# Half-size products for seven gate/up pairs, with weight sums made in DRAM

## The chip, the cores and the metric

The kernel runs on one NeuronCore of a Trainium2 chip. The metric is the device time of one execution in microseconds (us), given as the median of several runs. A profiled execution is one more run, recorded by the hardware profiler; its span, from the first to the last instruction, is what the profile's rows divide up. Engines are named as in the profile: PE is TensorE (matrix products), DVE is VectorE, ACT is ScalarE, POOL is GpSimd, SP is SyncE, whose queue issues nearly all transfers (DMAs). PEld is the loading of the stationary operand, which overlaps PE.

## The reference

One transformer block on 512 positions of width 1024, in fp32: normalize, project, attend in two ways (a sparse form with compressed, selected and windowed keys, and a sliding window with sinks), project, normalize, add; then the feed-forward part, which is what changes, and a gated addition at the end.

```python
h = rmsnorm(x, mlp_pre_g[i])
gu = h @ w_gate_up[i]                    # 1024 -> 2 x 2816
a, u = jnp.split(gu, [D_FF], axis=-1)
a = causal_dwconv(a, conv_w[i], conv_b[i])   # 3 taps along the positions
y = (jax.nn.gelu(a, approximate=True) * u) @ w_down[i]
x = x + rmsnorm(y, mlp_post_g[i])
e = p[i] @ w_ple[i]
x = x + e * jax.nn.sigmoid(x @ w_ple_gate[i])
```

## The kernel before

Everything is kept transposed: channels on the 128 partitions, the 512 positions along the free dimension (T = 512, H = 256, KC = 8 chunks of the model width, NFF = 22 tiles of the hidden width). A 32-bit product is made of three matmuls in a reduced 32-bit format (fp32r): each operand is split in a high part, a rounded copy made by ScalarE, and a low part, the difference, made by VectorE. The helper `mm3` (L149) issues high·high, low·high, high·low for one chunk of 128. The helper `weight` (L130) brings a weight tile of 128x1024 from DRAM (512 KB, on SP's queue, into a raw buffer "wr") and splits it (L134 on ScalarE, L138 on VectorE) into buffers "wh", of which there are six.

The program is written for a framework that assigns buffers and semaphores and orders each engine's instructions itself, by a simulated timeline; `prio`, `pin` and `keep_in_program_order` bend that order. The transfers of the SP queue share eight semaphores in rotation, so each waits until the one eight places before it has landed.

The stages in time: the input and its projections (to about 70 us); attention, in which the rest of the projections and the first half of the output projection run as fillers among the score and value products (`fill` at L180 is called once for each step of attention); output projection and norm (to about 279 us); gate/up (`mlp_up`, to about 494 us); down (`mlp_down`); the last norm and the gate.

Gate/up has 22 pairs j of tiles (gate and up, 24 matmuls of 512 columns each, 48 a pair). The input is not normalized beforehand: `self.h2` holds the un-normalized rows times the gain, split in high and low, and the normalization factor r3 (a row, spread over the partitions) is multiplied in behind the products, once for the gate tile (L1131, VectorE) and once for the up side (L1138, GpSimd). `mlp_tile` (below) does this with the three-tap convolution (L1134 to L1136), gelu (L1137), the product with the up tile (L1139) and the split of the result y (L1141, L1142). r3 itself is ready only after the first four tiles (`chunkwise`) and one more, so the first pairs queue up for it.

Down has eight output tiles c. Tiles 0 to 5 go as three pairs (`pair_of_tiles`): on the first 12 hidden tiles (6 pairs of them, KP = 6) a 2x2 block product is made with seven half-size products (Strassen's scheme: sums of weight blocks, sums of operand halves; 256 columns each), and the remaining ten hidden tiles go plainly. Tile 6 is plain, tile 7 is split in two halves of positions so that its norm can start early. The sums of operand halves are made by `sums` for the pairs of hidden tiles 0 to 3 (EARLY = 4) during gate/up, and by `sums_late` for the last two in down.

PSUM is eight banks of 128x512, handed out in rotation by tags ("mm" two, "s" three, "t" two, "o" one).

Of the kernel before, what the change touches and what calls it, by code (L numbers as in the profile page):

```python
# [64 lines left out]
EARLY = 4  # L65
MP = 3
ORDER = [[range(0, 4), (), range(4, 6)], [range(0, 3), range(3, 6), ()], [range(6), (), ()]]
TTAG = ["pt", "u", "u", "u", "p", "p", "p", "p"]
LAGS = [(1, 2), (2, 2)]


class Block:
# [76 lines left out]
    def mm3(self, ps, wt, off, x, start, stop, keep=False):  # L149
        mm = self.nc.tensor.matmul  # L150
        hi = wt[0][:, off : off + P]
# [5 lines left out]
        mm(ps, hi, x[:, 1, :], start=False, stop=stop)  # L157
# [876 lines left out]
    def sums(self, j, c):  # L1034

        nc = self.nc
        a, b = slice(0, H), slice(H, T)
# [4 lines left out]
        ta, tb = self.tt[j // 2]
        ra, rb = (self.sum[:, i, :] for i in range(2))
        if j % 2 == 0:
            nc.vector.tensor_sub(ra[:, a], c[:, b], c[:, a])
            nc.scalar.activation(rb[:, a], c[:, b], AF.Copy)
        else:
            nc.vector.tensor_sub(ra[:, b], c[:, b], ra[:, a])
            nc.vector.tensor_sub(rb[:, a], c[:, b], rb[:, a])
# [324 lines left out]
```

## Time and profile before

| what | us |
|---|---|
| median of three runs | 660.18 (659.74 to 660.29) |
| profiled execution, span | 657.9 |
| PE busy | 650.7 (99%) |
| DVE busy | 452.6 (69%) |
| ACT busy | 342.1 (52%) |
| POOL busy | 171.6 (26%) |
| share of PE in the chain that ended last | 93% |

A window row, as the prediction uses them, reads: the stretch and its length, then for PE, PEld, DVE, ACT and POOL the busy time and in brackets the number of instructions, then the granted TensorE clock, the busy share of the 16 DMA engines and the GB/s that they moved. A timeline row has the start, the duration, the engine, the line, the operation and what it writes and reads; in square brackets stands the idle time before it and who ended it. A row of a group has its busy time and the mean duration in ns behind the bar. A row on DMAs ends with the KB of each and the median us from issue to landing.

### The profile page before, as it was taken

What the parts mean: (1) busy time and instruction counts of PE and PEld (TensorE: products, weight loads), DVE (VectorE), ACT (ScalarE), POOL (GpSimd) and SP (SyncE); (2) the same over time, 40 slices, a digit from 0 to 9 for tenths busy, and PEclk for the clock granted to TensorE, in tenths of its full rate; (3) what the DMA queues carried; (4) which work ended last, traced back from release to release, by engine and by line L of the source; (5) the groups of instructions that cost most, each with busy time, mean ns of one, the idle gap of its engine ahead of it and who ended that gap; (6) DMA issues with size and microseconds to landing.
All of it is one profiled execution on the core that took longest, in us unless ns stands there. A gap on an engine that the chain in (4) does not pass through costs nothing.

```text
span 657.9 us, 9783 instructions
## 1 busy us (share of the span) xinstructions
PE 650.7 (99%) x3449; PEld 556.3 (85%) x3449; DVE 452.6 (69%) x965; ACT 342.1 (52%) x636; POOL 171.6 (26%) x248
## 2 busy tenths in 40 slices
PE   9999999999999999999999999999999999999997
PEld 8988878878888888888888888888889898989986
DVE  7795687978856469689876555555568857544873
ACT  7464687978887476346544333333334433342351
POOL 1111597677486060003211010101010002021000
PEclk9999999999999999999999999999999999999999
DMA  8436721212264437221242233222233332656032
GB/s 304 161 113 201 199 66 49 55 27 63 67 213 156 144 106 277 97 64 65 96 129 96 97 97 112 97 96 97 96 97 97 113 96 81 214 180 233 1 113 80
DMA packets 32129, 77.99 MB, mean 119 GB/s; under 512 B 3536, under 2 KB 11728, under 8 KB 32080
## 3 DMA queue, kind: packets, MB, share of 16 engines
q1 hardware_dynamic: 31936, 77.28, 36.7%
q8 instruction: 27, 0.44, 0.3%
q14 instruction: 22, 0.18, 0.1%
q10 hardware_dynamic: 144, 0.08, 0.0%
HBM read 63.72 MB, written 6.29 MB: 106 GB/s over the span
## 4 chain that ended last, share of the span: by engine, by line
PE 93%; DVE 4%; ACT 2%; POOL 1%; issue 1%; ACTq 0%; DVEq 0%
PE mlpup_pss L156 4%; PE mlpup_pss L153 4%; PE mlpup_pss L157 4%; PE mlpup_psmm L156 3%; PE mlpup_pst L156 3%; PE mlpup_psmm L153 3%; PE mlpup_pst L153 3%; PE mlpup_pst L157 3%; PE mlpup_psmm L157 3%; PE mlpdown_psmm L153 2%; PE mlpdown_psmm L157 2%; PE mlpdown_psmm L156 2%; PE mlpdown_pst L157 2%; PE mlpdown_pst L153 2%; PE mlpdown_pst L156 2%; PE nsa_pso L597 2%
## 5 line engine op out<-in xcount | busy, mean ns | idle before, releaser
L1138 POOL TENSOR_TENSOR mlpup_s<-mlpup_s,r3b 128x512 f32<-128x512 f32 x22 | 32.5, 1475 | 215.0 <-ACT mlpup_s L1137 215.0
L134 ACT ACTIVATE mlpup_wh<-mlpup_wr 128x1024 fp32r<-128x1024 f32 x38 | 40.1, 1057 | 61.8 <-PE mlpup_pss L156 27.6
L138 DVE TENSOR_TENSOR mlpup_wh<-mlpup_wr,mlpup_wh 128x1024 fp32r<-128x1024 f32 x38 | 46.4, 1222 | 4.5 <-ACT mlpup_wh L134 4.5
L153 PE MATMUL mlpup_pss<-r_u,mlpup_wh 128*128 128x512 f32 x120 | 46.7, 389 | 0.0
L156 PE MATMUL mlpup_pss<-r_u,mlpup_wh 128*128 128x512 f32 x120 | 46.7, 389 | 0.0
L157 PE MATMUL mlpup_pss<-r_u,mlpup_wh 128*128 128x512 f32 x120 | 46.7, 389 | 0.0
L587 POOL TENSOR_SCALAR nsa_u<-nsa_u,nsa_nrc,gate 128x512 f32<-128x512 f32 (+3 forms) x64 | 38.6, 615 | 14.7 <-DVE nsa_nrc L723 9.6
L134 ACT ACTIVATE mlpdown_wh<-mlpdown_wr 128x1024 fp32r<-128x1024 f32 (+2 forms) x22 | 21.3, 968 | 40.6 <-DMA mlpdown_wr<-in_down_dram 14.7
L689 ACT ACTIVATE nsa_u<-nsa_u,nsa_nnm 128x512 f32<-128x512 f32 (+3 forms) x64 | 35.4, 554 | 6.7 <-DVE nsa_nnm L682 6.6
L138 DVE TENSOR_TENSOR mlpdown_wh<-mlpdown_wr,mlpdown_wh 128x1024 fp32r<-128x1024 f32 (+2 forms) x22 | 24.4, 1111 | 20.7 <-ACT mlpdown_wh L134 20.7
L569 DVE TENSOR_TENSOR nsa_u<-nsa_pst,nsa_u 128x512 fp32r<-128x512 f32 (+1 forms) x43 | 29.4, 686 | 6.8 <-ACT nsa_u L566 6.5
L275 POOL TENSOR_TENSOR mlpdown_s<-mlpdown_s,mlpdown_s 128x512 f32<-128x512 f32 x6 | 9.8, 1630 | 93.0 <-ACT mlpdown_s L274 92.9
L138 POOL TENSOR_TENSOR fill_wh<-fill_wr,fill_wh 128x1024 fp32r<-128x1024 f32 (+2 forms) x13 | 24.6, 1896 | 26.5 <-ACT fill_wh L134 26.5
L1137 ACT ACTIVATE mlpup_s<-mlpup_s 128x512 f32<-128x512 f32 x22 | 13.9, 631 | 33.7 <-DVE mlpup_s L1136 33.7
L153 PE MATMUL mlpup_pst<-r_u,mlpup_wh 128*128 128x512 f32 x80 | 31.1, 389 | 0.0
L156 PE MATMUL mlpup_pst<-r_u,mlpup_wh 128*128 128x512 f32 x80 | 31.1, 389 | 0.0
L157 PE MATMUL mlpup_pst<-r_u,mlpup_wh 128*128 128x512 f32 x80 | 31.1, 389 | 0.0
L153 PE MATMUL mlpup_psmm<-r_u,mlpup_wh 128*128 128x512 f32 x80 | 31.1, 389 | 0.0
L156 PE MATMUL mlpup_psmm<-r_u,mlpup_wh 128*128 128x512 f32 x80 | 31.1, 389 | 0.0
L157 PE MATMUL mlpup_psmm<-r_u,mlpup_wh 128*128 128x512 f32 x80 | 31.1, 389 | 0.0
L682 DVE CUSTOM_DVE_ANT_0 nsa_u<-nsa_pss,biastables_u 128x224 f32<-128x224 f32 (+3 forms) x64 | 27.8, 446 | 3.0 <-PE nsa_pss L623 2.4
L566 ACT ACTIVATE nsa_u<-nsa_pst 128x512 fp32r<-128x512 f32 x43 | 25.4, 593 | 8.5 <-PE nsa_pst L564 7.9
(493 smaller groups left out, 2130.2 us busy)
## 6 DMA issues: line engine op xcount, KB each, us to landing
mlpup_wr<-in_gu_dram SPq DMA_DIRECT2D x38, 512.0 KB, 3.3
fill_wr<-in_win_dram SPq DMA_DIRECT2D x6, 512.0 KB, 3.7
mlpdown_u<-in_down_dram SPq DMA_DIRECT2D x11, 256.0 KB, 3.0
fill_u<-fill_u SPq DMA_DIRECT2D x20, 128.0 KB, 2.6
mlpdown_wr<-in_down_dram SPq DMA_DIRECT2D x5, 512.0 KB, 3.5
mlpdown_wr<-in_down_dram SPq DMA_DIRECT2D x6, 384.0 KB, 3.2
loadx_u<-in_xT_dram SPq DMA_DIRECT2D x8, 256.0 KB, 4.5
compress_u<-projk_u SPq DMA_DIRECT2D x16, 128.0 KB, 2.4
```

The costliest lines, as they stand in the source:

```text
L134: h = nc.scalar.activation(hi, raw, AF.Copy)
L138: l = eng.tensor_sub(lw, raw, hi.bitcast(F32))
L153: r = self.pin(mm(ps, hi, x[:, 0, :], start=start, stop=False))
L156: mm(ps, lo, x[:, 0, :], start=False, stop=False)
L157: mm(ps, hi, x[:, 1, :], start=False, stop=stop)
L566: nc.scalar.activation(t[:, 0, :], pt, AF.Copy)
L569: nc.vector.tensor_sub(t[rs, part, :], pt[rs], t[rs, 0, :].bitcast(F32))
L587: self.nc.gpsimd.tensor_scalar(ap, ap, col, gate, op0=ALU.mult, op1=ALU.mult)
L682: nc.vector.tensor_tensor_reduce(dst, src, dist, op0=ALU.add, op1=ALU.min, scale=SLOPES[8 + 4 * g + r], scalar=start, accum_out=out)
L689: nc.scalar.activation(dst, dst, AF.Exp, bias=nm[:, r, b : b + 1], scale=-1.0, accum_out=sm[:, r, b : b + 1])
L1137: nc.scalar.activation(c0, c0, AF.Gelu_apprx_tanh)
L1138: nc.gpsimd.tensor_mul(c0, c0, self.r3)
```

## The change

Seven of the gate/up pairs (j = 9, 11, ... 21) are computed by half-size products. For these, the four 4-chunk blocks of the pair (gate and up, first and second interleaved half of the input channels) and the two halves of the positions form a 2x2 block product with seven products of 4 chunks by 256 columns, 84 matmuls instead of 48 of 512 (`blocked_tile`). Further parts go with it:

- `normalized`: during the first gate/up tiles the input is multiplied by gain and r3 and split anew (`hn`), and the sums of its halves are made (`ht`). Tiles from j = 8 on use `hn` and no longer need the products with r3.
- The weight blocks come in a second layout of the same numbers (`gs`). Their sums are made in DRAM: 28 copies of 256 KB (four for each blocked pair) are issued on SP's queue during attention (`block_copies`), and 28 accumulating DMAs of 256 KB, two levels in a chain, on GpSimd's queue (`block_additions`).
- In down, the plain tile 6 comes first, and the operand sums of all six pairs are made there and in the first pair (`sums_of`); `sums`, `sums_late` are gone. The weights of the last gate are loaded behind the pairs.

```diff
-EARLY = 4
-ORDER = [[range(0, 4), (), range(4, 6)], [range(0, 3), range(3, 6), ()], [range(6), (), ()]]
+ORDER = [[range(0, 3), (), range(3, 6)], [range(0, 3), range(3, 6), ()], [range(6), (), ()]]
+BLOCKED = [9, 11, 13, 15, 17, 19, 21]
+ROWS = 2048
+RAW_LAST = 7
+COPY_FROM, COPY_STEP = 10, 3
...
         if self.loads:
             self.loads.pop(0)()
+        else:
+            self.calls += 1
+            if self.calls > COPY_FROM and self.calls % COPY_STEP == 0:
+                next(self.copies, lambda: None)()
...
+    def normalized(self, x1, kp):
+        f = self.u([P, 2, T])
+        for i in range(2):
+            k = 2 * kp + i
+            h = self.u([P, 2, T], F32R)
+            nc.vector.scalar_tensor_tensor(f[:, i, :], x1[kp][:, i, :], self.col(C_GMLP + k), self.r3, op0=ALU.mult, op1=ALU.mult)
+            nc.scalar.activation(h[:, 0, :], f[:, i, :], AF.Copy)
+            nc.vector.tensor_sub(h[:, 1, :], f[:, i, :], h[:, 0, :].bitcast(F32))
+            self.hn.append(h)
+            yield
+        t = self.u([P, 4, H])
+        parts = [self.u([P, 2, T], F32R, PTAG[2 * kp + i]) for i in range(2)]
+        self.half_sums([[f[:, i, hs] for hs in HALF] for i in range(2)], t, parts)
+        self.ht += parts
+        yield
+
+    def block_copies(self):
+        self.sums_in = [self.dp.tile([4, P, T], F32, name=f"blocks{i}") for i in range(len(BLOCKED))]
+        rows = lambda t: t.rearrange("p n -> (p n)").rearrange("(q e) -> q e", e=ROWS)
+        for i, d in enumerate(self.sums_in):
+            for k in range(4):
+                yield lambda i=i, d=d, k=k: self.load_late(rows(d[k]), rows(self.io["gs"][i, k]))
+
+    def block_additions(self):
+        nc, gs = self.nc, self.io["gs"]
+        rows = lambda t: t.rearrange("s p n -> s (p n)").rearrange("s (q e) -> q s e", e=ROWS)
+        add = lambda o, a: self.pin(nc.gpsimd.dma_start(rows(o), rows(a), accum_op=ALU.add, max_dma_last_dim=4 * ROWS))
+        for lo in range(0, len(BLOCKED), 2):
+            some = list(enumerate(self.sums_in))[lo : lo + 2]
+            for i, d in some:
+                yield lambda i=i, d=d: add(d[2:3], gs[i, 0:1])
+                yield lambda i=i, d=d: add(d[3:4], gs[i, 2:3])
+            for i, d in some:
+                yield lambda d=d: add(d[0:1], d[3:4])
+            for i, d in some:
+                yield lambda d=d: add(d[1:2], d[0:1])
+
+    def blocked_tile(self, j, tags):
...
+        plan = [
+            [(d[:, a], 0, x(0, a), True), (e[:, a], 4, x(1, a), True)],
+            [(f[:, b], 0, t(2), True), (g[:, b], 4, t(0), True)],
+            [(f[:, a], 0, t(1), False), (e[:, b], 4, x(1, b), False)],
+            [(g[:, a], 0, t(3), False)],
+        ]
+        for wt, products in zip(self.blocked_weights(j), plan):
+            for ps, first, op, begins in products:
+                for k in range(4):
+                    self.mm3(ps, wt, (first + k) * P, op(k), begins and k == 0, k == 3, shared=True)
+        q, v, w = self.s([P, T]), self.s([P, T]), self.s([P, T], tag="as")
+        nc.scalar.activation(q[:, a], d[:, a], AF.Copy)
+        nc.vector.tensor_sub(v[:, a], q[:, a], f[:, a])
+        nc.vector.tensor_add(v[:, b], v[:, a], f[:, b])
+        nc.vector.tensor_sub(q[:, b], v[:, a], g[:, b])
+        nc.vector.tensor_add(q, q, e)
...
+        self.conv(j, v, q)
+        nc.vector.tensor_mul(v, w, v)
+        self.keep_y(j, v)
...
     def mlp_down(self):
...
-        for c in range(0, 2 * MP, 2):
-            self.pair_of_tiles(c, yo[c // 2], acc)
         for c in range(2 * MP, KC - 1):
             m = yo[c // 2][:, c % 2, :]
             ps = self.ps("mm")
             for n, k in enumerate(ks):
                 wt = self.weight(io["down"][c][:, k.start * P : k.stop * P], len(k) * P)
                 self.gemm(ps, wt, [self.y[j] for j in k], k.start == 0, k.stop == NFF)
-                if n < 2:
-                    self.pgw.append(self.weight(io["wpg"][n], tag="u"))
+                self.sums_of(n)
...
+        for c in range(0, 2 * MP, 2):
+            self.pair_of_tiles(c, yo[c // 2], acc)
```

`sums_of(i)` adds the high and low parts of two hidden tiles (two additions of 512 columns), and `half_sums` makes four sums of 256 columns and splits them (two splits of 512).

How the order moves on three engines. First SP's queue in the attention stage, at about 59 to 73 us of the profile before. `fill_wr` are weight loads, `projq_u` moves of queries, `compress_u<-projk_u` the moves that fill the second half of the compressed keys, and `blocks` the DRAM buffers of the weight sums. Before:

```order
L146 DMA fill_wr_846<-in_win_dram 128x1024
L282 DMA projq_u_701<-projq_u_698 64x512 x4
L146 DMA fill_wr_1146<-in_win_dram 128x1024
L282 DMA compress_u_455<-projk_u_768 64x512 x2
L282 DMA compress_u_457<-projk_u_768 64x512
L282 DMA compress_u_456<-projk_u_768 64x512 x2
```

After:

```order
L156 DMA fill_wr_846<-in_win_dram 128x1024
L295 DMA blocks_975<-in_gs_dram 16x4096 x3
L298 DMA projq_u_701<-projq_u_698 64x512 x4
L295 DMA blocks_975<-in_gs_dram 16x4096
L295 DMA blocks_976<-in_gs_dram 16x4096
L156 DMA fill_wr_1159<-in_win_dram 128x1024
L295 DMA blocks_976<-in_gs_dram 16x4096 x2
L298 DMA compress_u_455<-projk_u_768 64x512 x2
L298 DMA compress_u_456<-projk_u_768 64x512 x2
```

Seven copies of 256 KB now stand ahead of the key moves, and the moves of tile 456 have come one place forward.

Second GpSimd, from the reciprocal root of the second norm on (r2c, at 243.94 in the profile before); the L1138 and, after, L1163 rows are the products with r3 for j = 0, 1, 2 and so on. Before:

```order
L222 TENSOR_TENSOR r2c<-r_rv_3059,mhalf 128x4
L1138 TENSOR_TENSOR mlpup_s_3347<-mlpup_s_3347,r3b 128x512
L1138 TENSOR_TENSOR mlpup_s_3363<-mlpup_s_3363,r3b 128x512
L1138 TENSOR_TENSOR mlpup_s_3406<-mlpup_s_3406,r3b 128x512
L1138 TENSOR_TENSOR mlpup_s_3472<-mlpup_s_3472,r3b 128x512
L1138 TENSOR_TENSOR mlpup_s_3552<-mlpup_s_3552,r3b 128x512
L1138 TENSOR_TENSOR mlpup_s_3630<-mlpup_s_3630,r3b 128x512
```

After, from the product for j = 3 to that for j = 5:

```order
L1163 TENSOR_TENSOR mlpup_s_3541<-mlpup_s_3541,r3b 128x512
L1199 DMA blocks_980<-in_gs_dram 32x2048 x2
L1199 DMA blocks_979<-blocks_979 32x2048
L1199 DMA blocks_980<-blocks_980 32x2048
L1199 DMA blocks_979<-blocks_979 32x2048
L1163 TENSOR_TENSOR mlpup_s_3646<-mlpup_s_3646,r3b 128x512
L1199 DMA blocks_980<-blocks_980 32x2048
L1199 DMA blocks_981<-in_gs_dram 32x2048 x2
L1199 DMA blocks_981<-blocks_981 32x2048 x2
L1163 TENSOR_TENSOR mlpup_s_3741<-mlpup_s_3741,r3b 128x512
```

Between these three products stand ten accumulating DMAs, and each `blocks<-blocks` waits for the one before it on the same buffer; twelve more stand between r2c and the product for j = 0, and six among the first products.

Third VectorE at the start of down, where the first two block weights (split in `mlpdown_wh` of 128x896) are made; L1058, L1131 to L1142 before are operand sums and the last hidden tiles. Before:

```order
L138 TENSOR_TENSOR mlpdown_wh_4841<-mlpdown_wr_4838,mlpdown_wh_4840 128x1024
L1142 TENSOR_TENSOR mlpup_u_4751<-mlpup_s_4744,mlpup_u_4751 128x512
L1131 TENSOR_TENSOR mlpup_u_3161<-mlpup_pss_4760,r3b 128x512
L1058 TENSOR_TENSOR mlpdown_s_4992<-mlpup_u_3875 128x512
L138 TENSOR_TENSOR mlpdown_wh_4875<-mlpdown_wr_4868,mlpdown_wh_4874 128x896
L1058 TENSOR_TENSOR mlpdown_s_4999<-mlpup_u_3948 128x512
L1058 TENSOR_TENSOR mlpdown_s_5008<-mlpup_u_4021 128x512
L1135 SCALAR_TENSOR_TENSOR mlpup_s_4817<-mlpup_u_3161,cols,mlpup_s_4817 128x512
L1136 SCALAR_TENSOR_TENSOR mlpup_s_4817<-mlpup_u_3161,cols,mlpup_s_4817 128x512
L138 TENSOR_TENSOR mlpdown_wh_4906<-mlpdown_u_4899,mlpdown_wh_4905 128x896
```

After:

```order
L148 TENSOR_TENSOR mlpdown_wh_5517<-mlpdown_wr_5510,mlpdown_wh_5516 128x896
L1153 TENSOR_TENSOR mlpup_u_5295<-mlpup_s_5282,mlpup_u_5295 128x512
L1062 TENSOR_TENSOR mlpdown_u_5382<-mlpdown_u_5383,mlpdown_u_5382 128x512
L1062 TENSOR_TENSOR mlpdown_u_5419<-mlpdown_u_5421,mlpdown_u_5419 128x512
L1062 TENSOR_TENSOR mlpdown_u_5420<-mlpdown_u_5421,mlpdown_u_5420 128x512
L1062 TENSOR_TENSOR mlpdown_u_5471<-mlpdown_u_5473,mlpdown_u_5471 128x512
L1062 TENSOR_TENSOR mlpdown_u_5472<-mlpdown_u_5473,mlpdown_u_5472 128x512
L1332 COPY mlpdown_u_5302<-mlpdown_psmm_5303 128x512
L148 TENSOR_TENSOR mlpdown_wh_5548<-mlpdown_u_5541,mlpdown_wh_5547 128x896
```

The splits of the operand sums (L1062) now stand between the first two block weights, behind the last hidden tile (5295).

More of the change, by code (lines that the diff above doesn't have):

```diff
@@ L1 @@
+import functools
 import itertools
@@ L95, in __init__ @@
         self.loads = []
+        self.calls = 0
+        self.copies = self.block_copies()
         self.pinned = None
@@ L156, in mm3 @@
         mm(ps, lo, x[:, 0, :], start=False, stop=False)
-        mm(ps, hi, x[:, 1, :], start=False, stop=stop)
+        self.last = mm(ps, hi, x[:, 1, :], start=False, stop=stop).ins
     def pin(self, r):
@@ L853, in attention @@
             self.fill_step()
+        for c in self.copies:
+            c()
         self.mix += [(mix[3][0][:, k, :], mix[3][1][:, k, :]) for k in range(2)]
@@ L1116, in pair_of_tiles @@
             plain(js)
+            if c == 0 and js is gs[0]:
+                for i in range(3, KP):
+                    self.sums_of(i)
             blocks(ks)
-            if c == 0 and js is gs[0]:
-                self.sums_late()
             if c == 2 * MP - 2 and len(ks):
@@ L1143, in mlp_tile @@
-        self.y.append(y)
-        if j < 2 * EARLY:
-            self.sums(j, c0)
+        c = self.s([P, T])
+        if j <= RAW_LAST:
+            a = self.s([P, T], tag="as")
+            nc.vector.tensor_mul(a, pa, self.r3)
+            self.conv(j, c, a)
+            nc.gpsimd.tensor_mul(c, c, self.r3)
+        else:
+            self.conv(j, c, pa)
+        nc.vector.tensor_mul(c, pu, c)
+        self.keep_y(j, c)
+    def normalized(self, x1, kp):
+        nc = self.nc
+        f = self.u([P, 2, T])
[12 more added lines that the diff above has]
+        yield
@@ new lines, in blocked_weights @@
+    def blocked_weights(self, j):
+        nc, i = self.nc, BLOCKED.index(j)
+        for src in (self.io["gs"][i, 0:2], self.sums_in[i][2:4], self.sums_in[i][0:2]):
+            yield self.weight(self.raw(src.rearrange("s p n -> p s n"), tag=next(self.rawtag)), early=True)
+        r = self.raw(self.io["gs"][i, 3], T, next(self.rawtag))
+        w = self.up.tile([P, D], F32R, tag="wh", name=self.nm("wh"), bufs=SLOTS["wh"])
+        hi, lo = (w[:, i * T : (i + 1) * T] for i in range(2))
+        nc.scalar.activation(hi, r[:, :T], AF.Copy)
+        nc.vector.tensor_sub(lo, r[:, :T], hi.bitcast(F32))
+        yield hi, lo
@@ L1167, in mlp_up @@
         nc, io = self.nc, self.io
-        am = self.u([P, 2, T + 2], F32, "kn")
-        self.am = [am[:, i, :] for i in range(2)]
-        for a in self.am:
-            nc.gpsimd.memset(a[:, 0:2], 0.0)
         self.y = []
         self.tt = []
-        ROT = self.ROT
+        self.hn, self.ht = [], []
+        x1 = self.x1
         pss = self.chunkwise(self.upw, self.h2, ("s", "mm", "s", "mm"))
@@ L1223, in mlp_down @@
         wts = []
-        for n, k in enumerate(ks):
-            wts.append(self.weight(io["down"][c][:, k.start * P : k.stop * P], len(k) * P))
-            if n == 0:
-                self.pgw.append(self.weight(io["wpg"][2], tag=("kn", "tt")))
+        for k, t in zip(ks, ("wr", "wr", "u")):
+            n = len(k) * P
+            wts.append(self.weight(self.raw(io["down"][c][:, k.start * P : k.stop * P], n, t), n, early=True))
+        for n, tag in enumerate((("p", "tt"), ("pt", "pt"), ("kn", "tt"))):
+            self.pgw.append(self.weight(io["wpg"][n], tag=tag))
         raw = self.raw(io["wpg"][3])
```

137 lines of the change are left out of this document (79 added, 58 removed).

## The prediction

> **What bounds the kernel now.** I read the engines' busy times first, then the chain that ended last, then the waits.
>
> ```profile
> span 657.9 us, 9783 instructions
> PE 650.7 (99%) x3449; PEld 556.3 (85%) x3449; DVE 452.6 (69%) x965; ACT 342.1 (52%) x636; POOL 171.6 (26%) x248
> PEclk9999999999999999999999999999999999999999
> PE 93%; DVE 4%; ACT 2%; POOL 1%; issue 1%; ACTq 0%; DVEq 0%
> PE x_psmm L303 <- DVE x_s L300: 1.5, 1, 1.5
> PE fill_psmm L863 <- POOL nsa_u L584: 0.3, 1, 0.3
> ```
>
> TensorE is busy for 650.7 of 657.9 us at the full granted clock, and its longest waits in the whole trace are 1.5 and 0.3 us. So time can only go by giving TensorE less to do, and a new wait of TensorE is added in full: no idle stretch swallows it later. For the same reason none of the costs bounded below can turn out a gain: there is no wait that could vanish. All sums below are made against this execution's span, 657.9; the median of the runs, 660.18, lies 2.3 above it, and I carry the difference over unchanged.
>
> **What the blocked pairs save.** The change replaces 48 matmuls of 512 columns by 84 of 256 in seven of the 22 gate/up pairs. Both shapes stand in the trace: 512 columns in the gate/up stage, 256 in the down stage's existing half-products. These two rows cover a stretch of each; the second count, PEld, is the number of weight loads, one for each matmul.
>
> ```profile
> 283.32:294.20 10.88, 10.88 (x49) 9.01 (x48) 8.97 (x13) 6.25 (x7) 1.30 (x1) 1.00 0.31 97
> 495.57:503.08 7.51, 7.51 (x64) 7.50 (x63) 7.48 (x17) 4.93 (x8) 0.00 (x0) 1.00 0.00 0
> ```
>
> 48 matmuls take 10.88 us, 0.2267 each; 63 half-width ones take 7.51, 0.1192 each, which is 53% and not 50%. Multiplication count alone promises an eighth of a pair, 1.36 us; the real saving is 10.88 − 84 × 0.1192 = 10.88 − 10.01 = 0.87 us, times seven **−6.1 us**. Nothing else on TensorE changes in number: the down stage does the same products in another order.
>
> **The r3 products that go** (14 on VectorE, 14 on GpSimd, for pairs 8 to 21) lie beside TensorE and are worth nothing in themselves: in steady state VectorE is busy 32, then 27 of 50 us (rows further down). The adds after each blocked pair (about 5.6 us of VectorE) and its four weight splits fit there: a blocked and a plain pair together need about 15 of VectorE's 20.9 us, and the four PSUM banks that a blocked pair takes come free a pair earlier. Cost 0.
>
> **The 28 copies on SP's queue.** They are put among the loads and moves of the attention stage, and seven of them stand ahead of the eight moves that fill the second half of the compressed keys (three after the load at 59.27, one before and one to three around the load at 65.10). Rows of SP's queue, of TensorE, and of the windows there (last two columns: share of the DMA engines, GB/s):
>
> ```profile
> 59.27 0.54 SPq L146 DMA_DIRECT2D fill_wr<-in_win_dram  x1
> 65.10 0.54 SPq L146 DMA_DIRECT2D fill_wr<-in_win_dram  x1
> 67.10 5.61 SPq L282 DMA_DIRECT2D compress_u<-projk_u  x8
> 72.70 0.40 PE L622 MATMUL nsa_pss<-compress_u,projq_u 128*128 128x512 f32 x1
> compress_u<-projk_u SPq DMA_DIRECT2D x8, 128.0 KB, 2.8
> 60.00:62.00 2.00, 2.00 (x12) 1.37 (x11) 0.60 (x1) 1.36 (x2) 1.07 (x1) 1.00 0.98 296
> 62.00:64.00 2.00, 2.00 (x10) 1.61 (x9) 1.97 (x2) 0.00 (x0) 1.33 (x1) 1.00 0.63 156
> 64.00:66.00 2.00, 2.00 (x10) 1.68 (x9) 1.54 (x6) 0.92 (x2) 0.00 (x0) 1.00 0.46 107
> 66.00:68.00 2.00, 2.00 (x10) 1.65 (x10) 1.41 (x2) 1.07 (x2) 0.00 (x0) 1.00 0.90 283
> 68.00:70.00 2.00, 2.00 (x11) 1.65 (x10) 0.41 (x1) 0.00 (x0) 0.00 (x0) 1.00 0.79 191
> 70.00:72.00 2.00, 2.00 (x12) 1.71 (x11) 1.53 (x6) 1.69 (x2) 0.77 (x1) 1.00 0.61 144
> 80.00:90.00 10.00, 9.75 (x60) 8.25 (x59) 7.88 (x44) 9.33 (x31) 9.35 (x16) 1.00 0.01 3
> ```
>
> The moves are issued from 67.10 on, 0.7 us apart, and land 2.8 us later. The score matmul at 72.70 reads two key tiles; their fourth half is the fifth move in line before, so it lands at about 67.1 + 4 × 0.7 + 2.8 = 72.7: no slack. After, it is the fourth, 0.7 us of slack. The DMA engines are free for 0.04 + 0.74 + 1.08 + 0.20 + 0.42 + 0.78 = 3.3 us between 60 and 72. At 0.90 share they moved 283 GB/s, so 314 at full share; a copy of 256 KB then takes 0.84 us of all engines if it costs what a load of that size does, and 1.7 if reading and writing DRAM count apart. Seven copies: 5.9 us against 3.3 free, 2.6 late, less 0.7: a **stall of 1.9 us**. No DRAM-to-DRAM row exists; the bounds are 0 (the three early ones go into the gap at 59 to 61 and the moves' waits for their sources hide the rest) and 7 × 1.7 − 3.3 − 0.7 = 7.9. I take 1.9, since the nearest rows are loads. The other 21 copies fall after these moves, where the engines rest (share 0.01 from 80 to 90) and the loads that they delay are needed later: 0.
>
> **The 28 accumulating DMAs on GpSimd's queue.** GpSimd runs in order. Twelve of them stand between the reciprocal root at 243.94 and the first r3 product, in 46 us in which GpSimd does nothing else: 0. The other 16 stand among the eight r3 products that stay, and there the second-level ones wait for the first to land.
>
> ```profile
> 243.94 1.95 POOL L222 TENSOR_TENSOR r2c<-r_rv,mhalf 128x4 f32<-128x4 f32 x1 [3.15 <-DVE r_rv L220]
> 292.53 1.30 POOL L1138 TENSOR_TENSOR mlpup_s<-mlpup_s,r3b 128x512 f32<-128x512 f32 x1 [46.65 <-ACT mlpup_s L1137]
> 303.96 1.31 POOL L1138 TENSOR_TENSOR mlpup_s<-mlpup_s,r3b 128x512 f32<-128x512 f32 x1 [2.55 <-ACT mlpup_s L1137]
> 340.55 0.69 DVE L1139 TENSOR_TENSOR mlpup_s<-mlpup_pst,mlpup_s 128x512 f32<-128x512 f32 x1 [2.07 <-POOL mlpup_s L1138]
> 348.61 0.39 PE L153 MATMUL mlpup_pss<-r_u,mlpup_wh 128*128 128x512 f32 x1
> kept_x<-outproj_u SPq DMA_DIRECT2D x2, 512.0 KB, 3.0
> kept_e<-pletiles_u SPq DMA_DIRECT2D x4, 512.0 KB, 7.2
> ```
>
> Between the fourth product (303.96 + 1.31 = 305.3) and the sixth stand ten of these DMAs with four waits for a landing in a row. With T from issue to landing and 0.54 us an issue (SP's, above) the sixth starts at 305.3 + 5.4 + 4T = 310.7 + 4T. VectorE then has its product with the up half and about 5.9 us of other rows before it splits the weight that TensorE takes at 348.61, so GpSimd may be as late as 348.6 − 5.9 − 0.7 − 1.3 = 340.7, which is T = 7.5. Stores to DRAM bound T: 3.0 to 7.2 us. Both ends are hidden; an accumulation also reads its target, so I do not exclude more. I take T = 5 and cost **0**, cover 10 us. [...]
>
> **VectorE from 279 to 355.** Here the pairs 0 to 7 still carry everything, and the normalized input and its half sums are added.
>
> ```profile
> 279.00:290.00 11.00, 11.00 (x50) 9.11 (x49) 10.47 (x11) 3.15 (x5) 0.00 (x0) 1.00 0.16 48
> 290.00:330.00 40.00, 40.00 (x178) 33.14 (x177) 36.23 (x54) 23.74 (x35) 11.13 (x6) 1.00 0.25 82
> 330.00:380.00 50.00, 50.00 (x222) 41.41 (x221) 32.33 (x43) 21.13 (x28) 6.71 (x5) 1.00 0.33 107
> 380.00:430.00 50.00, 50.00 (x223) 41.40 (x222) 27.00 (x35) 18.33 (x23) 6.46 (x5) 1.00 0.33 107
> L138 DVE TENSOR_TENSOR mlpup_wh<-mlpup_wr,mlpup_wh 128x1024 fp32r<-128x1024 f32 x36 | 44.0, 1222 | 3.0 <-ACT mlpup_wh L134 3.0
> L1135 DVE SCALAR_TENSOR_TENSOR mlpup_s<-mlpup_u,cols,mlpup_s 128x512 f32<-128x512 f32 x21 | 16.7, 795 | 0.3 <-ACT mlpup_s L1134 0.3
> L1142 DVE TENSOR_TENSOR mlpup_u<-mlpup_s,mlpup_u 128x512 fp32r<-128x512 f32 x20 | 13.7, 684 | 0.2 <-ACT mlpup_u L1141 0.2
> L1049 DVE TENSOR_TENSOR mlpup_u<-mlpup_s,mlpup_u 128x256 f32<-128x256 f32 x4 | 1.7, 414 | 0.0
> ```
>
> VectorE's load is 10.5 + 36.2 + half of 32.3 = 62.9 of 76 us. The sums of four early pairs go: 4 × (4 × 0.41 + 2 × 0.68) = 12.0. In come 8 scaled copies and 8 low parts, 8 × (0.80 + 0.68) = 11.8, and 16 half sums with 8 low parts, 16 × 0.41 + 8 × 0.68 = 12.1. Net +11.9: 74.8 of 76. Following its instructions in the changed order with these durations, the tightest weight (the one used at 348.6) is split about 2 us before. So there is cover, but a thin one: 0 to 3, taken **0.5 us**.
>
> **The start of down.** All six pairs' sums are now made here, 6 × (2 × 0.69 + 4 × 0.41 + 2 × 0.68) = 26 us of VectorE where before only two were late. The plain tile moved to the front and the first plain chunks cover it: about 87 matmuls, 19.7 us, plus 1 us until the first block's low weight is wanted; VectorE's 34 rows from the last blocked tile to that weight add up to about 20.6. Just in time, and then five low parts of sums (5 × 0.68) and a split of 896 columns, about 4.5 us, stand before the second block's weight, while a block gives TensorE 21 × 0.1192 = 2.5. That is 2 us late; the row at 495.57 above already shows VectorE at 7.48 of 7.51 in this place. Bounds 0 (the scheduler's order lets TensorE run ahead) and 4; taken **1.5 us**.
>
> The loads of the last projection's weights, moved behind the pairs, still have the split last tile as cover; the tail is 0.
>
> **Sum.** −6.1 + 1.9 + 0 + 0.5 + 1.5 = −2.2: span 655.7, median **658.0**.
>
> **Rivals.** (1) Everything is covered: 660.18 − 6.1 = 654.1. For it: each of the three stalls has 0 as its lower bound, and only the copies' one lies in a place where the moves land without slack. Against: VectorE at 75 of 76 us, and engines at 0.98, 0.90 and 0.79 share where the copies go. (2) The copies are dear: at 1.7 us each the stall at 72.7 is 7.9, and the time 660.2 − 6.1 + 7.9 + 2.0 = 664; from 5.4 us on it is slower than before beyond 0.2%, which I call the limit of what a measurement can tell. From 2.7 to 5.4 it shows no change. For it: TensorE uses the keys in the very moment at which they land. Against: the loads of this stage read DRAM and write elsewhere at 314 GB/s without paying twice. (3) The accumulations are slow. At T = 8.5 the sixth product starts at 344.7, 4 us late, VectorE stands behind it, TensorE behind VectorE's weight: 662; at T = 10 668. It decides from T = 8.4. For it: the landing of 7.2 us above; against: the other store row, 3.0, and a cover of 10 us at T = 5. [...] (4) The blocked matmuls do not reach 0.1192 because each product changes its bank: at 0.1296 the saving is 0, time 664 with the stalls; the down stage's half-products alternate banks at 0.1192, which speaks against it.
>
> **Chances.** Forecast, with 655.5 to 658.9 as its own range: 0.42. All covered: 0.17. Copies: 0.22, more than half of it no change, the rest slower. Accumulations: 0.15, nearly all slower. Half-products at no gain: 0.04, slower. Faster by over 0.2% is the first two, 0.59; within it 0.16; slower 0.25. The range runs from the covered case, less 0.4, to the copies' and the accumulations' dear cases, 664.
>
> **What the changed profile would show.** Blocked tiles at 10.0 us a pair; a wait of TensorE for a DMA of about 2 us near 72.7 (step two); no GpSimd product later than 340 and no VectorE wait for it over 2 us (step three); a wait of TensorE for VectorE under 1 us before 355 and of 1 to 2 us after the last blocked tile. The prediction is wrong if the first of these waits is absent (rival 1) or above 4 us (rival 2), or if GpSimd's sixth product starts after 345 (rival 3).

## The result: 0.7% slower, with five new waits

The changed kernel took 664.61 us (median of four runs, 662.78 to 666.63) against 659.96 of the kernel before in the same comparison; the ratio is 1.0071, 95% interval 1.0051 to 1.0091. The prediction, 658.0 with a range to 664.0, was too low, and it forecast a gain. Two things have to be explained: the profiled execution, whose span is 3.0 us longer than before (660.9 against 657.9), and the other runs, which are longer still at a lower clock:

| run of the changed kernel | time, us | span, us | mean granted clock |
|---|---|---|---|
| profiled | 662.78 | 660.9 | 1.000 |
| 2 | 664.60 | 662.8 | 0.996 |
| 3 | 664.62 | 662.8 | 0.996 |
| 4 | 666.63 | 664.7 | 0.994 |

The page of the changed kernel, its first lines and the chain that ended last:

```profile
span 660.9 us, 10545 instructions
PE 646.9 (98%) x3701; PEld 563.3 (85%) x3701; DVE 501.9 (76%) x1048; ACT 361.2 (55%) x667; POOL 174.3 (26%) x260
PEclk9999999999999999999999999999999999999999
PE 73%; DVE 15%; DMA 5%; ACT 3%; issue 2%; POOL 0%; SPq 0%; ACTq 0%; DVEq 0%
```

TensorE's busy time fell by 3.8 us only, and the chain leaves it for a quarter of the span: 15% of the chain is VectorE, where it was 4%. The waits of TensorE, by what it waited for, and then each in the timeline (start, duration, and in brackets the idle time and its end):

```profile
PE mlpdown_pss L168 <- DVE mlpdown_wh L148: 1.8, 2, 1.1
PE nsa_pss L638 <- DMA compress_u<-projk_u: 1.6, 1, 1.6
PE mlpup_pst L165 <- ACT mlpup_wh L144: 1.5, 1, 1.5
PE mlpup_psmm L168 <- DVE mlpup_wh L148: 1.3, 1, 1.3
```

```profile
74.27 0.47 PE L638 MATMUL nsa_pss<-compress_u,projq_u 128*128 128x512 f32 x1 [1.61 <-DMA compress_u<-projk_u]
331.05 0.50 PE L165 MATMUL mlpup_pst<-r_u,mlpup_wh 128*128 128x512 f32 x1 [1.49 <-ACT mlpup_wh L144]
349.65 0.50 PE L168 MATMUL mlpup_psmm<-mlpup_u,mlpup_wh 128*128 128x512 f32 x1 [1.34 <-DVE mlpup_wh L148]
515.41 0.38 PE L168 MATMUL mlpdown_pss<-mlpup_u,mlpdown_wh 128*128 128x256 f32 x1 [1.06 <-DVE mlpdown_wh L148]
547.18 0.39 PE L168 MATMUL mlpdown_pss<-mlpup_u,mlpdown_wh 128*128 128x256 f32 x1 [0.74 <-DVE mlpdown_wh L148]
```

None of these five stood in the profile before. The blocked pairs themselves do what was computed; this window holds the 84 matmuls of one of them:

```profile
396.69:406.71 10.02, 10.02 (x86) 10.02 (x84) 6.50 (x8) 5.71 (x7) 0.00 (x0) 1.00 0.49 156
```

10.02 us, against 10.88 for a plain pair: the 6.1 us are there. Going through TensorE's starts one by one and adding what each lies behind the usual pitch, the balance of the profiled execution is: attention +2.3 (the first matmul of gate/up starts at 252.37 instead of 250.06), the stalls in gate/up +3.7, those in down +2.5, small pieces +0.4, and −6.1: +2.8 of the measured +3.0.

### The profile page after: what moved, and what is told of

The parts are those of the page before. It is cut to its first block, busy times and chain, and to the rows that moved or that the text cites. A ratio compares the mean times of both kernels' runs of the same rounds, so it can differ in the third digit from the quotient of the medians.

```text
span 660.9 us, 10545 instructions
## 1 busy us (share of the span) xinstructions
PE 646.9 (98%) x3701; PEld 563.3 (85%) x3701; DVE 501.9 (76%) x1048; ACT 361.2 (55%) x667; POOL 174.3 (26%) x260
## 3 DMA queue, kind: packets, MB, share of 16 engines
q1 hardware_dynamic: 37536, 90.13, 41.7%
## 4 chain that ended last, share of the span: by engine, by line
PE 73%; DVE 15%; DMA 5%; ACT 3%; issue 2%; POOL 0%; SPq 0%; ACTq 0%; DVEq 0%
DMA mlpdown_wr<-in_down_dram 3%; PE mlpup_pss L168 3%; PE mlpup_pss L169 3%; PE mlpup_pss L165 3%; DVE mlpdown_wh L148 2%; PE nsa_pso L613 2%; DVE mlpup_s L1146 2%; PE nsa_pst L580 2%; PE mlpup_psmm L168 2%; PE mlpup_psmm L169 2%; PE mlpup_psmm L165 2%; PE mlpup_pst L169 2%; PE mlpup_pst L168 2%; PE mlpup_pst L165 2%; DVE mlpup_wh L148 2%
## 5 line engine op out<-in xcount | busy, mean ns | idle before, releaser
L144 ACT ACTIVATE mlpdown_wh<-mlpdown_wr 128x896 fp32r<-128x896 f32 (+2 forms) x27 | 26.3, 979 | 43.0 <-DMA mlpdown_wr<-in_down_dram 15.5
L148 DVE TENSOR_TENSOR mlpup_wh<-mlpup_wr,mlpup_wh 128x1024 fp32r<-128x1024 f32 x31 | 37.8, 1219 | 9.9 <-PE mlpup_psmm L168 4.7
L148 DVE TENSOR_TENSOR mlpdown_wh<-mlpdown_wr,mlpdown_wh 128x896 fp32r<-128x896 f32 (+2 forms) x27 | 31.2, 1163 | 9.3 <-ACT mlpdown_wh L144 8.8
L165 PE MATMUL mlpup_pss<-mlpup_u,mlpup_wh 128*128 128x256 f32 (+1 forms) x108 | 34.8, 322 | 0.1
L168 PE MATMUL mlpup_pss<-mlpup_u,mlpup_wh 128*128 128x256 f32 (+1 forms) x108 | 34.8, 322 | 0.0
L169 PE MATMUL mlpup_pss<-mlpup_u,mlpup_wh 128*128 128x256 f32 (+1 forms) x108 | 34.8, 322 | 0.0
L1146 DVE SCALAR_TENSOR_TENSOR mlpup_s<-mlpup_s,cols,mlpup_s 128x511 f32<-128x511 f32 (+1 forms) x30 | 27.3, 913 | 6.2 <-ACT mlpup_s L1144 6.0
L148 DVE TENSOR_TENSOR mlpup_wh<-mlpup_u,mlpup_wh 128x1024 fp32r<-128x1024 f32 x16 | 19.6, 1224 | 14.2 <-ACT mlpup_wh L144 11.2
L144 ACT ACTIVATE mlpup_wh<-mlpup_u 128x1024 fp32r<-128x1024 f32 x16 | 17.0, 1060 | 22.1 <-PE mlpup_pss L168 11.2
L168 PE MATMUL mlpup_psmm<-mlpup_u,mlpup_wh 128*128 128x256 f32 (+1 forms) x88 | 27.5, 313 | 1.3 <-DVE mlpup_wh L148 1.3
L169 PE MATMUL mlpup_psmm<-mlpup_u,mlpup_wh 128*128 128x256 f32 (+1 forms) x88 | 27.4, 312 | 0.0
L165 PE MATMUL mlpup_psmm<-mlpup_u,mlpup_wh 128*128 128x256 f32 (+1 forms) x88 | 27.4, 311 | 0.0
L613 PE MATMUL nsa_pso<-nsa_u,vnatural_u 128*128 128x512 f32 x72 | 25.8, 423 | 0.4 <-DVE nsa_s L597 0.2
L165 PE MATMUL mlpdown_psmm<-mlpup_u,mlpdown_wh 128*128 128x512 f32 (+1 forms) x76 | 26.0, 344 | 0.0
```

What stands on the lines that cost most here:

```text
L144: h = nc.scalar.activation(hi, raw, AF.Copy)
L148: l = eng.tensor_sub(lw, raw, hi.bitcast(F32))
L165: r = self.pin(mm(ps, hi, x[:, 0, :], start=start, stop=False))
L168: mm(ps, lo, x[:, 0, :], start=False, stop=False)
L169: self.last = mm(ps, hi, x[:, 1, :], start=False, stop=stop).ins
L613: self.att(nc.tensor.matmul(po, v, t[:, part, :], start=start, stop=stop))
```

## The experiments

Twelve kernels ran, three or five rounds each (one round for the middle chain). Spans are those of the profiled execution; the time is about 1.8 us more. One profile was kept of each, and one profile is a sample: four of these kernels (the changed one, the late copies, the other down order, no operand sums) give the engines the same instructions in the same order up to 480 us, and yet their stalls in gate/up came to 3.9, 3.5, 2.1 and 3.8 us. So what differs by 1 us between two single profiles need not be the work of an edit.

**Where the copies stand.** Each copy is tied, in order only, behind the attention matmul that was the last when it was written; no instruction of the other engines moves.

```diff
-                yield lambda i=i, d=d, k=k: self.load_late(rows(d[k]), rows(self.io["gs"][i, k]))
+                yield lambda i=i, d=d, k=k: self.copy_late(rows(d[k]), rows(self.io["gs"][i, k]))
+    def copy_late(self, dst, src):
+        r = self.nc.sync.dma_start(dst, src)
+        self.tc.keep_in_program_order(r)
+        self.tc.add_manual_dep(r.ins, self.steps[-1].name, mybir.DependencyInfo(
+            mybir.DependencyClass.NoSync, mybir.DependencyReason.DATA), reason="copy")
```

> Only the place of the 28 copies on SP's queue changes: each is tied behind the attention matmul that was last when it was written, so that none stands ahead of the key moves. Theory A: the wait near 74 vanishes, span 660.9 - 1.9 = 659.0. Rival: the copies collide with later loads and moves of attention instead, a new wait of 1 to 2 us there, span 660 to 661.

Measured: 660.95 us (ten runs, ratio to before 1.0019, 1.0010 to 1.0029), 3.7 us below the changed kernel. The wait for the keys is gone and gate/up starts at 249.85. But the profiled span is 660.2, since the stalls near 346 came to about 2.6 us instead of 2.0 and something else followed them. These windows of 2 us show it in the third column from the right, the granted clock:

```profile
346.00:348.00 2.00, 0.87 (x2) 0.78 (x3) 2.00 (x3) 1.96 (x3) 1.26 (x1) 0.72 0.00 0
348.00:350.00 2.00, 2.00 (x6) 1.54 (x6) 2.00 (x3) 0.80 (x2) 0.22 (x1) 0.50 0.82 246
350.00:352.00 2.00, 2.00 (x10) 1.60 (x9) 2.00 (x3) 0.33 (x1) 0.00 (x0) 0.93 0.57 166
```

Right after the stall TensorE ran at half its clock: 2 × (0.28 + 0.50 + 0.07) = 1.7 us of full-speed work lost, on top of the wait. The fastest of the ten runs (659.78 us, span 657.8) had a mean clock of 0.999; but the slowest, 662.17 us, had 1.000, so runs of one kernel differ by 2 us without the clock too. Their waits are not on record.

**Without weight sums, and without the accumulations alone.** Both leave out part of the computation, as their expectations say. The first also issues no copies and reads raw blocks (upper part of the edit); the lower part is common to both.

```diff
-        for src in (self.io["gs"][i, 0:2], self.sums_in[i][2:4], self.sums_in[i][0:2]):
+        for src in (gs[i, 0:2], gs[i, 2:4], gs[i, 1:3]):
...
-                    for _ in range(3):
-                        next(adds, lambda: None)()
```

> Leaves out the weight sums altogether: no copies, no accumulating DMAs, the blocked pairs read raw blocks. Theory A (copies delay the key moves by 1.9 us near 72; the accumulations' traffic and their waits in GpSimd's queue cause the two stalls at 331 and 350, 3.7 us): all three stalls vanish, span 660.9 - 1.9 - 3.7 = 655.3. Theory B (VectorE at 75 of 76 us causes the stall at 350 by itself): it stays, 656.6 or more. If the granted clock stays at 1.0 the time is 2 us above the span.

> Leaves out the 28 accumulating DMAs alone (the copies stay, sums stay unsummed). Theory A: the wait of 1.6 us near 74 stays, the two stalls at 331 and 350 vanish: span 657.2. Theory B (VectorE alone): the stall at 350 stays, span 658.6. No change (660.9) would say that the accumulations cost nothing.

Measured: 663.91 us without both (span 662.8, clock 0.994), 667.75 without the accumulations alone (span 665.6, clock 0.994). Theory A fell on the second stall. The first one did shrink; this is the kernel without the accumulations:

```profile
331.16 0.50 PE L168 MATMUL mlpup_pst<-r_u,mlpup_wh 128*128 128x512 f32 x1 [0.47 <-DVE mlpup_wh L148]
```

0.47 instead of 1.49, and the weight loads around it say why. The time from issue to landing (minimum, median, maximum) between 315 and 331, in the changed kernel and then without the accumulations:

```profile
DMA to landing us min/median/max: 3.3/4.0/6.7
```

```profile
DMA to landing us min/median/max: 3.1/3.2/3.3
```

The accumulations do not hold up GpSimd's products, which the prediction had worked out; they move on the same 16 DMA engines as the weight loads (6.2% of the engines' span for GpSimd's queue, 41.7% for SP's, in the changed kernel's page), and beside them one load took 6.7 us to land, against 3.3 at most without them. The stalls between 300 and 340 came to 1.3 to 1.9 us in the four profiles with accumulations named above and to 0.8 in these two without, so the cost is 0.5 to 1 us. But the second stall, at the first blocked pair, came to more than before: without any sums TensorE arrives there about 3 us earlier, and waits.

```profile
346.55 0.50 PE L165 MATMUL mlpup_psmm<-mlpup_u,mlpup_wh 128*128 128x512 f32 x1 [2.22 <-ACT mlpup_wh L144]
```

VectorE's windows (the third busy time in a row) in the changed kernel, then without sums:

```profile
290.00:330.00 40.00, 39.56 (x175) 32.38 (x173) 39.64 (x55) 22.42 (x32) 18.59 (x20) 1.00 0.75 163
330.00:350.00 20.00, 17.51 (x76) 14.04 (x77) 20.00 (x30) 13.02 (x19) 7.13 (x5) 1.00 0.62 198
```

```profile
290.00:330.00 40.00, 39.52 (x175) 32.33 (x174) 38.64 (x56) 23.71 (x34) 8.50 (x5) 1.00 0.22 72
330.00:350.00 20.00, 16.54 (x71) 13.02 (x70) 20.00 (x29) 11.58 (x17) 7.54 (x3) 0.94 0.44 161
```

VectorE has hardly any idle time left from 290 to 350 in either (59.6 and 58.6 of 60 us busy). It splits the weights, and by that frees the raw buffers into which SP loads the next (in the changed kernel the loads of L156 waited for the gate/up splits 41 times, 158.2 us in all); so it seems that what TensorE gains ahead of this stretch is given back at its end, which the next run puts to the test. (In these two kernels up to 25 of VectorE's rows also stand in another place, and the clock fell to half for 6.8 us in a row, so their totals are not to be read closely.)

**More time for VectorE.** On top of the late copies, the normalized input is used from j = 10 and only six pairs are blocked.

```diff
-BLOCKED = [9, 11, 13, 15, 17, 19, 21]
+BLOCKED = [11, 13, 15, 17, 19, 21]
-RAW_LAST = 7
+RAW_LAST = 9
```

> On top of the late copies: the normalized input is used two tiles later (from j = 10) and six pairs are blocked (11, 13, ... 21), so VectorE gets 22 us more for the same normalization work. Theory C (the stalls at 322 to 348 come from VectorE's full queue between 279 and 352, which also frees the raw weight buffers late): they vanish, 3.4 us, and 0.9 of saving is given up: span 657.9 at full clock - 3.4 + 0.9 = 655.4. Rival (the blocked weights' own loads, bunched on SP's queue, are late whenever blocking begins): a stall of 2 us or more just before the first blocked pair, then near 370: span 657.5 or more.

Measured: 659.62 us (ten runs; ratio 0.9993, 0.9982 to 1.0004), span 657.5. The mechanism is confirmed, the total is not: in gate/up no stall is left,

```profile
290.00:330.00 40.00, 40.00 (x178) 33.13 (x177) 39.97 (x57) 23.73 (x34) 16.52 (x17) 1.00 0.72 158
330.00:350.00 20.00, 20.00 (x90) 16.57 (x89) 20.00 (x29) 10.53 (x15) 5.65 (x3) 1.00 0.55 197
```

with VectorE just as full, and the accumulations still running, TensorE is busy for all 60 us. The first blocked pair now comes after VectorE's work and not before it. Yet three waits in down remain (1.2, 1.0 and 1.5 us behind the pitch; the last is new).

**Down.** One kernel leaves out the operand sums (on the changed kernel), one, on the late copies, changes the order in the first pair.

```diff
-        f = self.u([P, 2, T], F32, STAG[i])
...
+        self.tt.append(self.y[2 * i : 2 * i + 2])
```

> Leaves out the operand sums in down (the block products read the hidden tiles in place of the sums): 26 us of VectorE and the ScalarE splits go. Theory A (VectorE's queue at the start of down causes the stalls at 515 and 547): both vanish, span 660.9 - 2.3 = 658.6 or lower. Rival for the second: at 547 the block weights come late by their loads and by GpSimd's square sum at the same time, not by the operand sums; it stays, span 659.7.

```diff
-ORDER = [[range(0, 3), (), range(3, 6)], [range(0, 3), range(3, 6), ()], [range(6), (), ()]]
+ORDER = [[(), (), range(6)], [range(0, 3), range(3, 6), ()], [range(6), (), ()]]
```

> On top of the late copies: in the first down pair all three plain chunks come before the six block products (instead of one chunk, three blocks, two chunks, three blocks). The first block weight is wanted 36 matmuls, 8.2 us, later. Theory: the stall of 1.2 us at 514 vanishes; the one of 1.0 at 546 (second pair, loads and GpSimd's square sum) stays: span 1.2 below that of the late copies. Rival: VectorE has the same sum of work before the last block of the pair, so the stall only moves there: no change.

Measured: without the operand sums both stalls in down are gone, so the sums cause both, with VectorE as the engine that TensorE waits for, and the rival falls (ScalarE's splits of the sums went with them; their share was not tried). Its time, 663.55 (span 661.9), does not show that, because its stall at the keys was 2.77 us this time and the clock fell behind it:

```profile
75.78 0.47 PE L638 MATMUL nsa_pss<-compress_u,projq_u 128*128 128x512 f32 x1 [2.77 <-DMA compress_u<-projk_u]
78.00:80.00 2.00, 2.00 (x8) 1.71 (x6) 1.42 (x8) 1.58 (x4) 1.20 (x3) 0.50 0.82 211
```

The other order: 659.71 us (ratio 1.0001, 0.9989 to 1.0013), 1.2 us less than the late copies alone (ratio 1.0019). The waits in down fell from 2.2 to 1.0 us.

**The clock.** The kernel before, with TensorE made to wait six times in gate/up; nothing of the change is in it. The matmuls of all gate/up tiles are also kept in program order, which moves nothing ahead of the first gap.

```diff
+STALLS = (8, 10, 12, 14, 16, 18)
+CHAIN = 3
...
-            self.ordered = n < 4
+            if i == 0 and j in STALLS:
+                self.stall()
+            self.ordered = True
...
+    def stall(self):
+        t = self.s([P, P], F32R)
+        nc.vector.memset(t.bitcast(F32), 0.0)
+        ps = self.ps("o")
+        for _ in range(CHAIN):
+            keep(nc.tensor.matmul(ps[:, :P], t, t, start=True, stop=True))
+            keep(nc.scalar.activation(t, ps[:, :P], AF.Copy))
+        keep(nc.tensor.matmul(ps[:, :P], t, t, start=True, stop=True))
```

> The kernel before with TensorE made idle six times in gate/up (ahead of tiles 8, 10, ... 18) by a chain of four small matmuls that wait for three ScalarE copies, some 2 to 3 us each. Theory D (a stall of about 2 us makes the granted clock drop to half for about 4 us afterwards, as the trace of the late copies and of the other two shows after theirs): the time rises by the six waits plus about 2 us after most of them, mean clock 0.98. Rival (the drops have another cause, such as the half-width products): the time rises by the waits alone and the clock stays at 1.0.

> As the run with six stalls, but each chain has two small matmuls and one copy, about 1 us each. Theory D with a threshold between 1 and 2 us: the time rises by the waits alone, about 6 us, clock at 1.0. If short waits also drop the clock: 12 us or more, clock 0.99 or below.

> The kernel before with six stalls, as in the two runs with long and short chains, each chain of three small matmuls and two copies, gaps of about 2.1 us. If a gap must fill about half of a window of 3.4 us to drop the clock (none of five gaps of 1.4 did, about half of those of 2.8 did): none or one or two of the six drop it, the time is the gaps plus 0 to 4 us. If the threshold is above 2.1: none.

| chain | gaps in TensorE's full-width stream, us | span − 657.9 | not explained by the gaps | gaps followed by half clock |
|---|---|---|---|---|
| 3 copies | 5.35, then 5 × 2.80 | 26.2 | 6.9 | 4 of 6 |
| 2 copies | 4.68, then 5 × 2.11 | 18.1 | 2.9 | the first |
| 1 copy | 2.81, then 5 × 1.41 | 12.7 | 2.8 | the first |

Four drops at 1.7 us are 6.8 of the 6.9 us that the gaps leave open. With two copies the half clock lasted 6.8 us, with TensorE idle in a part of them. With one copy 1.7 us are the drop and 0.7 were lost ahead of gate/up; 0.4 stay open. So Theory D holds in these three runs, in a stage that has no half-width product: a gap cost its length and, in six of the 18 cases, half clock after it as well, 1.7 us for each drop of one step.

Which cases, the traces tell. In all 14 profiles of this study the granted clock changes only at whole multiples of 3.413 us from its first change, so the time is cut into clock steps of that length. In the long chain the drops begin at 342.52, 369.82, 421.02 and 472.22, which are 8, 15 and 15 steps apart. These rows are such steps: the one that holds the second gap and the one behind it, then the two that share the third gap and the one behind them:

```profile
366.40:369.82 3.42, 1.66 (x8) 1.14 (x7) 2.52 (x3) 2.10 (x5) 0.27 (x1) 1.00 0.02 8
369.82:373.23 3.41, 3.41 (x9) 2.64 (x9) 0.00 (x0) 0.00 (x0) 0.00 (x0) 0.50 0.40 145
390.30:393.71 3.41, 2.51 (x12) 1.88 (x10) 1.34 (x3) 1.78 (x4) 1.29 (x1) 1.00 0.48 154
393.71:397.12 3.41, 2.54 (x11) 1.96 (x12) 1.77 (x2) 1.05 (x4) 0.00 (x0) 1.00 0.36 107
397.12:400.54 3.42, 3.42 (x17) 2.83 (x16) 0.00 (x0) 0.00 (x0) 0.00 (x0) 1.00 0.12 47
```

Two equal gaps, one followed by half clock and one not: the second lies within one step, the third is spread over two. With every matmul counted at its usual pitch (an estimate from the starts in the traces), TensorE was idle for 2.6 us of the first of these steps, and for 1.1 and 1.6 us of the two others. Of all full-clock steps between 45 and 635 us in the 14 profiles, twelve were followed by half clock; they had 2.0 us of idle time or more (the least is 2.03), and no other step had more than 1.98. That 1.98 is the second stall of the changed kernel's own profile, which escaped a drop by little. So in these profiles not the length of a gap decides alone, but how much idle time falls into one step, and where the steps lie differs from run to run. None of the gaps of 2.11 and 1.41 us behind the first was followed by a drop. For 2.11 the place is enough to explain it: these five lie about 7 steps apart and were split between two steps each time.

A drop lasts about 3.4 us here, or a multiple of it, but a gap need not be that long: one of 1.94 us behind the pitch (1.78 us in the timeline, in the run with the other down order, at 329) was enough, in a step with 2.07 us idle.

**Together.** Late copies, six pairs from j = 11, the other order in down; then two variants: seven pairs, all but the last one pair later (10, 12, 14, 16, 18, 20 and 21, RAW_LAST = 8), and, with six pairs, the third pair of down reordered too (its last entry `[(), range(6), ()]`). The first variant's expectation says that a plain tile comes last. That is not what its edit does: pairs 20 and 21 are both blocked, one right behind the other.

> Late copies, six pairs blocked from j = 11, and in the first down pair all plain chunks ahead of the six block products. The run with six pairs had three waits left, all in down (1.2, 1.0 and 1.5 us); the run with the other down order had 1.0 in place of 2.2 there. If the gains add: span 657.5 - 1.2 to 657.5 - 3.7, that is 654 to 656.3, median about 657. Rival (VectorE has too much work in down in whatever order, so the waits only move): no better than six pairs alone, span 657.5.

> Late copies, the other down order, seven pairs blocked at 10, 12, ... 20 and the normalized input from j = 9: one pair later than in the changed kernel, all of the saving kept, and a plain tile last. If one pair (11 us of VectorE's time) is enough, the stalls before the first blocked pair vanish: span 657.9 - 6.1 + 1 to 2 left in down = 653 to 654. If two pairs are needed, a stall of 1 to 2 us stays near 340 and half of the runs lose 2 us more by the clock: 655 to 657.

> As the run with late copies, six pairs and the other down order, and in the third down pair the first two plain chunks come before the block products. If the wait of 1.5 us near 572 is there in that run, it vanishes here: 1.5 us less. If it is gone there already: no difference.

Measured, five rounds each: 658.27 us (nine runs, 656.95 to 659.47; ratio to before 0.9976, 0.9967 to 0.9986); 660.98 (ratio 1.0016); 663.37 (ratio 1.0052). The first is faster than both kernels of this study. Its span is 655.7 and its clock 0.999 to 1.000 in all runs; the gains of the two parts add, less than in full. These are its largest waits:

```profile
PE x_psmm L326 <- DVE x_s L323: 1.5, 1, 1.5
PE mlpdown_pss L168 <- DVE mlpdown_wh L148: 0.5, 1, 0.5
PE mlpdown_pss L165 <- ACT mlpdown_wh L144: 0.4, 1, 0.4
```

The seven pairs have no stall in gate/up either (0.3 us at most), so one pair, 11 us, was enough for VectorE there. But down begins with a wait of 2.70 us for ScalarE's weight at 523, and ScalarE had waited for VectorE's sums of weight blocks:

```profile
522.50 0.95 ACT L144 ACTIVATE mlpdown_wh<-mlpdown_wr 128x896 fp32r<-128x896 f32 x1 [3.03 <-DVE mlpdown_wr L1089]
```

Half clock follows from 523.3 to 526.7 in the profile, and the mean clock is 0.995 to 0.997 in every one of the eleven runs. VectorE is busy for all of the 3.4 us before that, and two blocked pairs in a row ahead of down leave it more to do at this point; that this is the reason was not tried.

The reordered third pair made the end worse, where its expectation saw no difference: the sums of its squares came late, and TensorE waited 2.4 us at 603 for them. In the third pair itself a wait of 1.3 us appeared at 581.

## Why the prediction was wrong, point by point

- **The blocked pairs, −6.1.** Right: 10.02 us for 84 matmuls against the 10.01 computed from the down stage's rows. The rival that half-products gain nothing is out.
- **The copies, +1.9.** Right in place, and near in size: a wait of 1.61 and one of 0.31 for the key moves, gate/up starts 2.3 later, and putting the copies behind the moves takes it back. The size is in part luck. In two other profiles with the copies in this place the longer wait was 2.1 and 2.8 us. And the working, DMA engines without free time, did not come true as it stands: between 62 and 70 they still had 1.7 us free, while the first key move was issued at 68.54 instead of 67.10 and landed after 5.2 us instead of 4.0. How much of the wait is SP's issuing and how much the engines was not separated. No run shows the price of 0.84 us for a copy.
- **The accumulations in GpSimd's queue, 0.** The queue was covered, as forecast. GpSimd had issued the tenth of these DMAs by 335.2; by 310.7 + 4T that is T = 6.1, above the 5 that was taken and below the 7.5 that was allowed. The landings had medians of 7.2 and 5.0. GpSimd's instructions started in the program's order, each product behind the DMAs ahead of it: the sixth at 336.92, behind the DMA at 334.41. It then still waited for ScalarE, and took 4.29 us instead of 1.3:

```profile
334.41 0.76 POOL L1199 DMA_DIRECT2D blocks<-blocks  x1 [4.37 <-DMA blocks<-blocks]
336.92 4.29 POOL L1163 TENSOR_TENSOR mlpup_s<-mlpup_s,r3b 128x512 f32<-128x512 f32 x1 [1.74 <-ACT mlpup_s L1147]
blocks<-in_gs_dram POOLq DMA_DIRECT2D x14, 256.0 KB, 7.2
blocks<-blocks POOLq DMA_DIRECT2D x14, 256.0 KB, 5.0
```

  The sign that no product comes later than 340 failed all the same: the two last ones started at 345.35 and 349.26, held up by ScalarE and not by an accumulation. What the step left out is the traffic: it was costed for GpSimd alone and not for the weight loads beside it, one of which took 6.7 us to land; 0.5 to 1 us at 331. With VectorE busy for 64.6 of the 65 us from 290 to 355, the accumulations issued from 290 to 340 landed after 3.9 to 7.2 us.
- **VectorE from 279 to 355, +0.5.** This is the step that failed: a cover of about 2 us and a stall of 0 to 3, taken as 0.5, where TensorE stalled for 3.7 us. The sum for VectorE, 74.8 of 76 us, is itself too small. For the time from 330 to 355 it took half of the row from 330 to 380. This row of the profile before covers the stretch as it is:

```profile
279.00:355.00 76.00, 76.00 (x337) 62.94 (x336) 64.68 (x89) 38.64 (x55) 15.26 (x9) 1.00 0.28 90
```

  That is 64.68 and not 62.9, and with the net +11.9 it makes 76.6 of 76: no cover at all, before any row takes longer than its mean. In the changed kernel VectorE was busy for 64.6 of the 65 us from 290 to 355. The durations were means over a whole stage. Among the rows that they price too low are two-operand steps that run beside a GpSimd product. The one below overlaps for 1.24 us with the product that started at 336.92 and took 1.78 us; the 58 of its kind from 250 to 500 that overlap with none took 0.69 to 0.75, with a median of 0.74:

```profile
339.97 1.78 DVE L1146 SCALAR_TENSOR_TENSOR mlpup_s<-mlpup_s,cols,mlpup_s 128x511 f32<-128x511 f32 x1
```

  From 290 to 350 seven rows of this kind (five of the convolution, two of the new scaled copies) took 1.5 to 1.8 us each, 7.1 us more together than at 0.74. The profile before has two of them, 2.1 us, which its window held already; so 5.0 us of VectorE's time were in no sum. They are a part of the load and not the cause alone: the run with six pairs has the same seven and no stall. That the full queue is the cause is shown by the run with six pairs: with the first blocked pair behind VectorE's extra work instead of in front of its end, the 3.7 us are gone. Between 0.5 and 1 us of them is the accumulations'.
- **The start of down, +1.5.** The mechanism was right and the size too small: 2.5 us, with a second stall in the second pair, which the prediction had not followed so far.
- **The sum and the clock.** Every unknown was priced as a wait, once. In twelve places of the 14 profiles half clock followed a wait of TensorE, up to 1.7 us of full-speed work lost for each 3.4 us of it. The profiled run had none of it; its three companions are 1.9, 1.9 and 3.8 us longer at 0.996, 0.996 and 0.994, which fits one and two such drops. Their traces are not on record, so longer waits may have a part in it. The median lies 4.65 us above that of the kernel before: 2.8 of it the profiled run has too (662.78 against 659.96), the waits less the savings, and 1.8 goes with the lower clock. No rival had this, and the range ended at 664.0 because each rival took one mechanism alone.

## What to carry to other kernels

Where one engine is the bound, the work it is relieved of is the smaller part of a prediction: count what the others must do in the same stretch, and treat an engine at 98% of a stretch, by mean durations, as the new bound. Take its load from the stretch itself and not from half of a longer one. A stall is not only its length: in the 14 profiles here, each full-clock step of 3.413 us from 45 to 635 us in which TensorE was idle for 2.03 us or more was followed by half clock, at a loss of up to 1.7 us for each step of it. So a change that trades matmuls for several short waits can lose even if its saving on TensorE comes out as computed. The place of the new work (two pairs later, 28 copies behind the moves, plain chunks first) decided the sign here, 1.0071 against 0.9976 with one blocked pair less.

## What was not expected of the hardware

Half clock for about 3.4 us followed single gaps of TensorE of 1.94 to 2.9 us in some cases, and in others gaps of 2.1 to 2.8 did not bring it; about 2.0 us of idle time within one clock step of 3.413 us separates them in all 14 profiles. In the changed kernel a 256 KB accumulating DMA within DRAM landed after 5.0 us in the median where source and target are buffers, after 7.2 where the source is the input, and GpSimd was busy with an issue for 0.76 to 1.95 us, the longer ones where several follow each other. A plain copy of 256 KB within DRAM took 5.5 us in the median. A load of 512 KB beside accumulations took up to 7.7 us between 300 and 331, and 3.1 to 3.3, from 315 to 331, where they were left out.
